# Inverting DeltaNet's 32x32 blocks: rounds of doubling on TensorE in place of a substitution fed through DRAM, with the heads paced

## The chip, the cores and the metric

The kernel runs on one core of a Trainium2 chip. The metric is the device time of one execution in microseconds; the time before is the median of three runs. The profile is that of one execution.

## The reference, cut to what matters

One layer of a diffusion backbone, all in float32: 512 latent tokens and 256 context tokens, width 2048. The tokens are normed and modulated, go through one wide input projection, and feed two mixers of eight heads each. The mixers' results are normed, gated, projected, merged and projected again; a mixture of sixteen experts follows.

The change lies in the second mixer (gated DeltaNet), of which the core is this, for each head and chunk:

```
diff = G[..., :, None] - G[..., None, :]
gamma = jnp.where(incl, jnp.exp(jnp.where(incl, diff, 0.0)), 0.0)
kk = jnp.einsum('bhik,bhjk->bhij', k, k)
m = eye + jnp.where(strict, beta[..., :, None] * kk * gamma, 0.0)
sol = lax.linalg.triangular_solve(m, rhs, left_side=True, lower=True, unit_diagonal=True)
```

What the chunk's state and output need is the inverse of a triangular matrix with ones on its diagonal. The scan runs in both directions, context first.

## The kernel before

The kernel goes through these stages in order: constants and norms; the value projection; per head the first mixer (`hgrn_in`, `hgrn`, with `ada_block` between); then a woven stage with the second mixer's eight heads; `branches` and `merge`; `project`; router; experts.

**The chunks of the second mixer.** The kernel uses chunks of 128 tokens: six (four latent, two context), two directions, so twelve 128x128 triangular matrices N for each head. Their inverse is built in three levels: the 32x32 blocks on the diagonal, then 64x64, then 128x128. The blocks of 32 are kept packed: `uc` (the inverse) and `utc` (its transpose) are tiles of [128, 12, 32], four blocks of 32 rows for each of twelve matrices.

**How a block of 32 is inverted before.** In `gdn_solve`, VectorE packs the 16x16 diagonal blocks into `nk` (two instructions), SyncE's queue stores `nk` to DRAM (`n_d`, 96 KB) and loads it back spread over partitions (`big`, 1536 KB); VectorE then substitutes row by row: 15 times a product `m` and a difference on `ut`. Two scalings by `par` and a transpose give `utc` and `uc` with blocks of 16 inverted. GpSimd has masked `ncm` with `umask`. One step from 16 to 32 follows on TensorE, in the helper `blocks`: 48 small matmuls (32x32 each, every one of two passes in float32, one in each quarter of the array) into a PSUM tile `mx`, copied by ScalarE to `w1`; then two more `blocks`, for `uc` and for `utc`, each subtracted by VectorE.

**The weave.** TensorE's order in this stage is written by the program (`manual_schedule`); the other engines' orders are made by the framework. `weave` holds generators, called streams here: for each head `s_in` (load k, v, q, transposes, norms), `s_solve` (the inverse), two `s_chain` (the scan over six chunks, one for each direction) and `s_out`. A stream yields a distance, or a condition. The distance is counted on `self.pe`, a planner's clock that each matmul moves: `mm` adds its columns, times four in float32, and at least 80, over 2400; `tr` adds 0.107. While no stream is due, one filler step is put in. `fill` gives 640 such steps: 40 products of the input projection (eight `job_gb`, 32 `job_gate`), each 48 matmuls of 512 columns, three to a step (0.64 on the planner's clock). When the filler is used up, the planner's clock jumps to the next due stream and TensorE's order holds nothing in between. The first `pre` filler steps are put ahead of the streams. Filler that is left after the weave is put ahead of the merge, with the loading of its operands (`branches`).

A head's `s_solve` needs its `s_in` and the solve before it; its second half needs the chain before it (`yield free`); a chain needs its solve and the chain before it. The chains of one head thus run beside the next head's solve. The PSUM tiles of solve and chains are all `mx`, of which there are two; the transposes and N use `pcx`, three.

The filler's weights come as `wraw` over SyncE's queue and are split into `whi` (ScalarE) and `wlo` (GpSimd).

Of the kernel before, what the change touches and what calls it, by code (L numbers as in the profile page):

```python
# [8 lines left out]
F32 = mybir.dt.float32  # L9
F32R = mybir.dt.float32r  # L10
I32 = mybir.dt.int32
AF = mybir.ActivationFunctionType
OP = mybir.AluOpType
# [8 lines left out]
H = 8  # L22
# [15 lines left out]
def view(t, off, dims, p0=0, n=128):  # L38
    ps = t.ap[0][0]
    return bass.AP(tensor=t.tensor, offset=t.offset + p0 * ps + off, ap=[[ps, n]] + [list(d) for d in dims])  # L40


class Kern:
# [44 lines left out]
    def consts(self):  # L88
        nc = self.nc
# [3 lines left out]
        tp = self.pool("ctmp", side="right")  # L93
# [3 lines left out]
        def c(name, shape, dt=F32):  # L97
            return (cp if name in late else fp).tile(shape, dt, name=name)

        V = nc.vector  # L100
# [31 lines left out]
        V.tensor_tensor(x32, p31, ii[:, :32], op=OP.bitwise_xor)  # L132
        self.dmask = c("dmask", [128, 32])
        V.tensor_scalar(self.dmask, x32, 0.0, None, op0=OP.is_equal)
        self.lmask = c("lmask", [128, 5, 32], I32)
        t1 = tp.tile([128, 32], F32, name="t1")
        t2 = tp.tile([128, 32], F32, name="t2")
        for n in range(5):
# [1 line left out]
            V.tensor_scalar(t1, x32, float(b), None, op0=OP.is_ge)  # L140
            V.tensor_scalar(t2, x32, float(2 * b), None, op0=OP.is_lt)
            V.tensor_tensor(self.lmask[:, n], t1, t2, op=OP.mult)

        self.umask = c("umask", [128, 32])
        V.tensor_scalar(self.umask, x32, 16.0, None, op0=OP.is_ge)
        self.par = c("par", [128, 2])
        V.tensor_scalar(self.par[:, 1:2], p31[:, 0:1], 16.0, None, op0=OP.is_ge)
        V.tensor_scalar(self.par[:, 0:1], p31[:, 0:1], 16.0, None, op0=OP.is_lt)
        sh2 = tp.tile([128, 16], I32, name="sh2")
        V.tensor_scalar(sh2, pi[:, :16], 15, None, op0=OP.bitwise_and)  # L150
        self.del16 = c("del16", [128, 16])
        V.tensor_tensor(self.del16, sh2, ii[:, :16], op=OP.is_equal)
        self.sel = c("sel", [128, 32])
        V.tensor_tensor(self.sel, p31, ii[:, :32], op=OP.is_equal)

# [230 lines left out]
    def head_norm_steps(self, pool, z, gain, extra, dst, wait=6):  # L386

        nc = self.nc
        V, S = nc.vector, nc.scalar
        sq = pool.tile([128, NL], F32, name="tmp", bufs=4)  # L390
        S.activation(sq, z, AF.Square)
        yield self.opt.get("lm", 1.6)
        pm = self.px.tile([128, NL], F32, name="mx")
        for c in range(4):
            self.mm(pm[:, c:c + 1], sq[:, c * 128:c * 128 + 128], self.ones[:, 0:1])
        ms = pool.tile([128, 4], F32, name="hms")
        rs = pool.tile([128, 4], F32, name="hrs")
        V.tensor_scalar(ms, pm[:, 0:4], 1.0 / 128, EPS, op0=OP.mult, op1=OP.add)
        self.rsqrt(pool, rs, ms)
        yield wait  # L400
        pm = self.px.tile([128, NL], F32, name="mx")
        for c in range(4):
            self.mm(pm[:, c * 128:c * 128 + 128], rs[:, c:c + 1].to_broadcast([128, 128]), self.ident)
        y = sq
        V.scalar_tensor_tensor(y, z, gain, pm, op0=OP.mult, op1=OP.mult)
        if extra is not None:
            V.tensor_tensor(y, y, extra, op=OP.mult)
        nc.scalar.dma_start(dst, y)
# [328 lines left out]
    def gdn_solve(self, h, R, Z, free, after):  # L737
# [2 lines left out]
        V, S, G = nc.vector, nc.scalar, nc.gpsimd  # L740
        kT, qT = R["kT"], R["qT"]
        gm, qe = R["gm"], R["qe"]
        lc = self.opt.get("lc", (2.0, 2.0, 1.6, 4.0, 1.6, 2.5, 1.6, 2.5))
        N = p.tile([128, 2, 6, 128], F32, name="N")
        for i0, w in ((0, 4), (4, 2)):
            pt = self.pt4()
            for i in range(w):
                self.mm(pt[:, i], kT[:, i0 + i], kT[:, i0 + i])
            for d in range(2):
                for i in range(w):  # L750
                    c = i0 + i
                    V.scalar_tensor_tensor(N[:, d, c], pt[:, i], self.beta[:, c, d * 8 + h:d * 8 + h + 1],  # L752
                                           gm[:, d, c], op0=OP.mult, op1=OP.mult)
            yield lc[0]
        P = p.tile([128, 2, 4, 128], F32, name="P", bufs=2)
        pt = self.pt4()
        for i in range(4):
# [4 lines left out]
            self.gdn_decay(after)  # L762
        yield lc[1]

        Nf = N.rearrange("p d c i -> p (d c) i")
        C = lambda n: p.tile([128, 12, 32], F32, name=n)
        ncm, uc, utc, w1 = C("ncm"), C("uc"), C("utc"), C("w1")
        for q in range(4):
            r = slice(32 * q, 32 * q + 32)
            V.tensor_copy(ncm[r], Nf[r, :, r])  # L770
        nk = p.tile([128, 12, 16], F32, name="nk")
        V.tensor_scalar(nk, ncm[:, :, 0:16], self.par[:, 0:1], None, op0=OP.mult)
        V.scalar_tensor_tensor(nk, ncm[:, :, 16:32], self.par[:, 1:2], nk, op0=OP.mult, op1=OP.add)
        nd = self.n_d[h]
        nc.sync.dma_start(nd, nk.rearrange("p c s -> p (c s)"))
        B = p.tile([128, 16, 12, 16], F32, name="big")
        nc.sync.dma_start(B.rearrange("p r c s -> p (r c s)"),
                          bass.AP(tensor=nd.tensor, offset=nd.offset, ap=[[3072, 8], [0, 16], [1, 3072]]))
        ut = p.tile([128, 2, 6, 16], F32, name="ut")
        V.tensor_copy(ut.rearrange("p d c s -> p (d c) s"), self.del16[:, None, :].to_broadcast([128, 12, 16]))  # L780
        m = p.tile([128, 2, 6, 16], F32, name="m")
        for w in range(15, 0, -1):

            mo = m[:, :, :, :w]
            V.tensor_tensor(mo, view(B, w, [[(16 - w) * 192 + 96 + 15 - 2 * w, 2], [16, 6], [192, w]]),
                            view(ut, w, [[96 + 15 - 2 * w, 2], [16, 6], [0, w]]), op=OP.mult)
            uo = view(ut, 0, [[96 + 16 - w, 2], [16, 6], [1, w]])
            V.tensor_tensor(uo, uo, mo, op=OP.subtract)
        utf = ut.rearrange("p d c s -> p (d c) s")
        for a in range(2):  # L790
            V.tensor_scalar(utc[:, :, a * 16:a * 16 + 16], utf, self.par[:, a:a + 1], None, op0=OP.mult)
        fl = lambda t: t.rearrange("p c s -> p (c s)")
        V.transpose(fl(uc), fl(utc))

        nm = ncm
        G.tensor_tensor(nm, ncm, self.umask[:, None, :].to_broadcast([128, 12, 32]), op=OP.mult)

        def blocks(lhs, rhs):
            po = self.ptile("s", [128, 12, 32])
            for i in range(12):  # L800
                for q in range(4):
                    r = slice(32 * q, 32 * q + 32)
                    self.mm(po[r, i], lhs[r, i], rhs[r, i])
            return po

        yield self.opt.get("ls", 32)
        S.activation(w1, blocks(nm, utc), AF.Copy)
        yield lc[2]
        p1 = blocks(w1, uc)
        p2 = blocks(uc, w1)  # L810
        V.tensor_tensor(uc, uc, p1, op=OP.subtract)
        V.tensor_tensor(utc, utc, p2, op=OP.subtract)
        yield lc[3]
        yield free

        U, UT = self.U, self.UT
        w2 = p.tile([128, 6, 32], F32, name="w1")
        pw = self.ptile("s", [128, 6, 32])
        hv = [(d, t + 32 * d, t + 32 * (1 - d)) for t in (0, 64) for d in range(2)]
        for c in range(6):  # L820
# [18 lines left out]
            V.tensor_scalar(UT[i:i + 32, d, :, o:o + 32], p2[i:i + 32], -1.0, None, op0=OP.mult)  # L839
        yield lc[5]  # L840

        w3 = p.tile([128, 6, 64], F32, name="w1")
        pw = self.ptile("s", [128, 6, 64])
        hv = [(d, 64 * d, 64 * (1 - d)) for d in range(2)]
        for c in range(6):
# [13 lines left out]
    def gdn_chain(self, h, d, R, Z, po, seen):  # L859
# [5 lines left out]
        for n in range(6):  # L865
            c = (FWD, BWD)[d][n]
            X = R["vtm"][:, c]
            if n:
                pk = self.ptile("pk", [128, 128])
                self.mm(pk, R["kT"][:, c], st)  # L870
                X = p.tile([128, 128], F32, name="X", bufs=2)
                V.scalar_tensor_tensor(X, pk, self.neG[:, c, hd:hd + 1], R["vtm"][:, c], op0=OP.mult, op1=OP.add)
                yield self.opt.get("lx", 1.0)
            pv = self.ptile("pv", [128, 128])
            self.mm(pv, Z["U"][:, d, c], X)
            a = po[:, c * 128:c * 128 + 128] if c < 4 else None
# [3 lines left out]
            if c < 4:  # L880
# [1 line left out]
                S.activation(vb, pv, AF.Copy, scale=self.beta[:, c, hd:hd + 1])  # L882
                self.mm(a, st, Z["qe"][:, d, c], start=sum(seen) == 0, stop=False)
                seen[c] += 1
            yield self.opt.get("lv", 1.0)
            if n < 5:
                pu = self.ptile("pu", [128, 128])
                self.mm(pu, R["ktm"][:, c], vs)
# [6 lines left out]
            if c < 4:  # L895
                self.mm(a, vb, Z["P"][:, d, c], start=False, stop=seen[c] == 3)
                seen[c] += 1
            yield self.opt.get("lu", 1.0)

    def gdn_out(self, h, po):  # L900
        nc, p = self.nc, self.gp
# [350 lines left out]
    def blocks(self, pr):  # L1252


        w = self.opt.get("lb", (512, 512, 512, 256, 256)) if pr == E // 2 - 1 else (D,)
        return [slice(sum(w[:i]), sum(w[:i + 1])) for i in range(len(w))]
# [207 lines left out]
    def run(self):  # L1464
# [4 lines left out]
        self.y_d = [dp.tile([128, 8, NL], F32, name=f"y_d{i}") for i in range(2)]  # L1469
        self.c_d = [[dp.tile([128, NT + 2], F32, name=f"c_d{h}_{i}") for i in range(3)] for h in range(H)]  # L1470
        self.G_d = dp.tile([16, NT], F32, name="G_d")
        self.n_d = [dp.tile([128, 192], F32, name=f"n_d{i}") for i in range(H)]
        self.mg_d = [dp.tile([128, NL], F32, name=f"mg_d{i}") for i in range(32)]
        self.b_d = [dp.tile([128, NL], F32, name=f"b_d{i}") for i in range(H)]
        self.row_d = [dp.tile([128, D], F32, name=f"row_d{i}") for i in range(2)]
# [43 lines left out]
        filler = self.fill(jobs + gates[3 * len(hs):])  # L1519
        man = self.tc.manual_schedule(engines={mybir.EngineType.PE})  # L1520
        man.__enter__()
        for _ in range(opt.get("pre", 110)):
            next(filler, None)
        n = len(hs)
        did = set()

        def s_in(i):
            yield lambda: i < 1 or ("in", i - 1) in did
            yield from self.gdn_in(hs[i], R[hs[i]], lambda: i < 2 or ("chain", i - 2) in did)
            did.add(("in", i))  # L1530

# [75 lines left out]
```

## Time and profile before

| What | Value |
|---|---|
| median of 3 runs | 3430.93 us (3427.51 to 3434.18) |
| profiled execution | 3427.16 us |
| its span, first to last instruction | 3425.1 us |
| mean granted TensorE clock | 0.963 |
| TensorE busy | 3177.2 us (93%) |
| VectorE busy | 1502.3 us (44%) |
| ScalarE, GpSimd busy | 860.7 us, 367.9 us |

A share of busy time is a mean over stages with different limits. A busy TensorE is not one at its peak: matmuls overlap, so the length of one in the rows (0.39 us for 512 columns) is longer than the distance from one to the next. Float32 matmuls of the streams appear as two records each, one for each pass. In the timeline a bracket at the end of a line gives the idle time ahead of it and what ended that.

### The profile page before, as it was taken

To read this page: it belongs to the slowest core of one execution; us is meant where nothing else is said; L and a number is where in the kernel's file an instruction comes from. 1 tells how busy PE (TensorE), PEld (TensorE's weight loads), DVE (VectorE), ACT (ScalarE), POOL (GpSimd) and SP (SyncE) were. 2 spreads that over 40 slices of the span, in tenths; PEclk is the share of its full clock that TensorE was granted. 3 is DMA by queue.
4 is the path that set the end of the run, shared out by engine and by line. 5 is a ranking of instruction groups with operands and counts; after the bars stand their busy time and mean duration, and the time that the engine had idled before them with its cause. 6 is when DMAs were issued, how large, how long until landed. Compare 5 with 4: busy or idle time off the path is not lost.

```text
span 3425.1 us, 52531 instructions
## 1 busy us (share of the span) xinstructions
PE 3177.2 (93%) x22034; PEld 2301.4 (67%) x22034; DVE 1502.3 (44%) x3101; ACT 860.7 (25%) x1556; POOL 367.9 (11%) x303
## 2 busy tenths in 40 slices
PE   6999999999999989888888779999799999999997
PEld 5788888888888767666766658778544444444443
DVE  5325576676677524455545545423311111211113
ACT  4322323232232224333333322223111010000102
POOL 0000000010000233222222201100000000000002
PEclk9999999999999989899999979999899999999998
DMA  9943264455455435344444325532789999999998
GB/s 305 244 124 117 85 205 152 135 179 159 143 173 166 139 110 135 94 103 103 110 105 110 88 88 151 194 120 71 296 335 420 420 420 420 420 421 420 421 420 308
DMA packets 456268, 738.90 MB, mean 216 GB/s; under 512 B 21723, under 2 KB 332211, under 8 KB 405983
## 3 DMA queue, kind: packets, MB, share of 16 engines
q1 hardware_dynamic: 427503, 688.12, 58.2%
q10 hardware_dynamic: 28528, 47.43, 3.9%
q8 instruction: 173, 2.83, 0.3%
q14 instruction: 64, 0.52, 0.0%
HBM read 703.16 MB, written 32.32 MB: 215 GB/s over the span
## 4 chain that ended last, share of the span: by engine, by line
PE 54%; DMA 7%; DVE 5%; ACT 1%; issue 1%; SPq 0%; ACTq 0%; DVEq 0%
PE pu L80 12%; PE pl L80 11%; PE pg L80 7%; PE px L80 6%; PE po L80 5%; DMA big<-n_d 5%; PE pb L80 5%; PE mx L80 4%; PE py L80 2%; PE pcx L85 1%; DMA rw<-in_router_w 1%; PE pcx L80 1%; DMA yraw<-y_d 0%; DVE N L752 0%; PE lg L80 0%
## 5 line engine op out<-in xcount | busy, mean ns | idle before, releaser
L80 PE MATMUL pl<-hlh,whi 128*128 128x512 f32 (+1 forms) x1552 | 637.1, 411 | 1.7 <-ACT whi L348 1.0
L80 PE MATMUL pl<-hll,whi 128*128 128x512 f32 (+1 forms) x1552 | 617.1, 398 | 0.0
L80 PE MATMUL pl<-hlh,wlo 128*128 128x512 f32 x1536 | 612.9, 399 | 3.7 <-DVE wlo L350 1.8
L348 ACT ACTIVATE whi<-wraw 128x1024 fp32r<-128x1024 f32 (+1 forms) x280 | 289.6, 1035 | 869.5 <-PE pl L80 197.0
L350 DVE TENSOR_TENSOR wlo<-wraw,whi 128x1024 fp32r<-128x1024 f32 (+1 forms) x200 | 256.6, 1284 | 283.9 <-ACT whi L348 283.7
L80 PEld LDWEIGHTS pl<-hlh,whi 128*128 128x128 f32 (+1 forms) x1552 | 295.7, 191 | 59.8 <-ACT whi L348 1.4
L80 PEld LDWEIGHTS pl<-hlh,wlo 128*128 128x128 f32 x1536 | 293.4, 191 | 48.6 <-DVE wlo L350 3.2
L80 PEld LDWEIGHTS pl<-hll,whi 128*128 128x128 f32 (+1 forms) x1552 | 295.6, 190 | 36.0 <-issue 0.7
L80 PE MATMUL pg<-ew,xs 128*64 128x512 f32 x992 | 249.0, 603 | 0.0
L350 POOL TENSOR_TENSOR wlo<-wraw,whi 128x1024 fp32r<-128x1024 f32 x80 | 193.5, 2418 | 490.2 <-ACT whi L348 434.6
L994 DVE SCALAR_TENSOR_TENSOR aacc<-awt,sc,aacc 128x512 f32<-128x512 f32 x256 | 209.6, 819 | 77.0 <-DMA awt<-in_ada_w 68.4
L80 PE MATMUL pu<-ew,xs 128*64 128x512 f32 x1000 | 242.4, 600 | 0.0
L1342 DVE TENSOR_TENSOR xo<-xo,px 128x512 f32<-128x512 f32 (+1 forms) x116 | 76.8, 668 | 360.6 <-PE px L80 360.6
L80 PE MATMUL py<-ew,aa 128*64 128x512 f32 (+1 forms) x608 | 230.1, 583 | 0.0
L80 PE MATMUL pu<-ew,aa 128*64 128x512 f32 x448 | 199.4, 592 | 0.0
L80 PEld LDWEIGHTS pu<-ew,xs 128*64 128x64 f32 x1000 | 88.9, 136 | 122.8 <-issue 115.5
L80 PEld LDWEIGHTS pg<-ew,xs 128*64 128x64 f32 x992 | 87.4, 137 | 120.9 <-issue 112.8
L80 PE MATMUL pcx<-hch,whi 128*128 128x256 f32 (+1 forms) x528 | 149.9, 284 | 0.0
L80 PE MATMUL pcx<-hcl,whi 128*128 128x256 f32 (+1 forms) x528 | 149.0, 282 | 0.0
L80 PE MATMUL pcx<-hch,wlo 128*128 128x256 f32 x512 | 145.8, 285 | 0.0
L80 PEld LDWEIGHTS pu<-ew,aa 128*64 128x64 f32 x448 | 61.5, 137 | 118.3 <-issue 118.3
L80 PEld LDWEIGHTS px<-oh,x 128*128 128x128 f32 x1024 | 125.6, 199 | 7.9 <-DVE xo L1342 4.0
(463 smaller groups left out, 4844.7 us busy)
## 6 DMA issues: line engine op xcount, KB each, us to landing
ew<-in_w_up SPq DMA_DIRECT2D x125, 1024.0 KB
ew<-in_w_gate SPq DMA_DIRECT2D x124, 1024.0 KB
ew<-in_w_down SPq DMA_DIRECT2D x124, 1024.0 KB
wraw<-in_w_in SPq DMA_DIRECT2D x208, 512.0 KB
awt<-in_ada_w SPq DMA_DIRECT2D x128, 512.0 KB
aw<-in_ada_w SPq DMA_DIRECT2D x32, 1024.0 KB
big<-n_d SPq DMA_DIRECT2D x8, 1536.0 KB
wraw<-in_w_out SPq DMA_DIRECT2D x24, 512.0 KB
```

Source lines behind the costliest of these rows:

```text
L80: self.nc.tensor.matmul(out, lhsT, rhs, start=start, stop=stop, skip_group_check=True)
L85: self.nc.tensor.transpose(out, in_, self.ident[:n, :n])
L348: nc.scalar.activation(hi[:, :n], raw[:, :n], AF.Copy)
L350: eng.tensor_tensor(lo[:, :n], raw[:, :n], hi[:, :n].bitcast(F32), op=OP.subtract)
L994: V.scalar_tensor_tensor(acc, w[:, k], self.sc[:, k0 + k, 0:1], acc, op0=OP.mult, op1=OP.add)
L1342: V.tensor_tensor(xo[t][:, cs], (x1 if pr == 0 else xo)[t][:, cs], pz[:, :n], op=OP.add)
```

## The change

The 32x32 blocks are inverted by doubling from 2 to 32. For each level n the part of N that joins two blocks of size 2^n is masked out (`nm[:, n]`; level 0 by VectorE, levels 1 to 4 by GpSimd). Level 0 gives `uc` as identity minus mask, without a product. Each of the four following levels is a round: `blocks(nm[:, n], utc)`, copied by ScalarE to `w1`; `blocks(w1, uc)`, subtracted from `uc` by VectorE, which then transposes `uc` into `utc`. The packing into `nk`, its store, the load of `big`, the substitution and the distance `ls` of 32 are gone. The masks are made ahead of P, where before the packing came behind it.

Beside this, distances are changed: in the solve (`lc`), in the chains (`lx`, `lv`, `lu`) and in the head norm (`lm`). `pre` goes from 110 filler steps to 40. `s_in` of head i also waits until the planner's clock is 70 i past its start.

```diff
@@ consts
-        self.lmask = c("lmask", [128, 5, 32], I32)
+        self.lmask, self.gmask = c("lmask", [128, 5, 32], I32), c("gmask", [128, 5, 32])
...
-        self.umask = c("umask", [128, 32])
-        V.tensor_scalar(self.umask, x32, 16.0, None, op0=OP.is_ge)
-        self.par = c("par", [128, 2])
...
-        V.tensor_tensor(self.del16, sh2, ii[:, :16], op=OP.is_equal)
+            V.tensor_tensor(self.gmask[:, n], t1, t2, op=OP.mult)
@@ head_norm_steps
-        yield self.opt.get("lm", 1.6)
+        yield self.opt.get("lm", 2.2)
@@ gdn_solve
-        lc = self.opt.get("lc", (2.0, 2.0, 1.6, 4.0, 1.6, 2.5, 1.6, 2.5))
+        lc = self.opt.get("lc", (2.4, 4.0, 2.0, 2.6, 2.0, 3.0, 2.0, 3.0))
...
             yield lc[0]
+
+        Nf = N.rearrange("p d c i -> p (d c) i")
+        C = lambda n: p.tile([128, 12, 32], F32, name=n)
+        ncm, uc, utc = C("ncm"), C("uc"), C("utc")
+        for q in range(4):
+            r = slice(32 * q, 32 * q + 32)
+            V.tensor_copy(ncm[r], Nf[r, :, r])
+        nm = p.tile([128, 5, 12, 32], F32, name="nm")
+        fl = lambda t: t.rearrange("p c s -> p (c s)")
+        V.tensor_tensor(nm[:, 0], ncm, self.gmask[:, 0][:, None, :].to_broadcast([128, 12, 32]), op=OP.mult)
+        for n in range(1, 5):
+            G.tensor_tensor(nm[:, n], ncm, self.gmask[:, n][:, None, :].to_broadcast([128, 12, 32]), op=OP.mult)
+
+        V.tensor_tensor(uc, self.dmask[:, None, :].to_broadcast([128, 12, 32]), nm[:, 0], op=OP.subtract)
+        V.transpose(fl(utc), fl(uc))
         P = p.tile([128, 2, 4, 128], F32, name="P", bufs=2)
...
         yield lc[1]
 
-        Nf = N.rearrange("p d c i -> p (d c) i")
-        C = lambda n: p.tile([128, 12, 32], F32, name=n)
-        ncm, uc, utc, w1 = C("ncm"), C("uc"), C("utc"), C("w1")
-        for q in range(4):
-            r = slice(32 * q, 32 * q + 32)
-            V.tensor_copy(ncm[r], Nf[r, :, r])
-        nk = p.tile([128, 12, 16], F32, name="nk")
-        V.tensor_scalar(nk, ncm[:, :, 0:16], self.par[:, 0:1], None, op0=OP.mult)
-        V.scalar_tensor_tensor(nk, ncm[:, :, 16:32], self.par[:, 1:2], nk, op0=OP.mult, op1=OP.add)
-        nd = self.n_d[h]
-        nc.sync.dma_start(nd, nk.rearrange("p c s -> p (c s)"))
-        B = p.tile([128, 16, 12, 16], F32, name="big")
-        nc.sync.dma_start(B.rearrange("p r c s -> p (r c s)"),
-                          bass.AP(tensor=nd.tensor, offset=nd.offset, ap=[[3072, 8], [0, 16], [1, 3072]]))
-        ut = p.tile([128, 2, 6, 16], F32, name="ut")
-        V.tensor_copy(ut.rearrange("p d c s -> p (d c) s"), self.del16[:, None, :].to_broadcast([128, 12, 16]))
-        m = p.tile([128, 2, 6, 16], F32, name="m")
-        for w in range(15, 0, -1):
-
-            mo = m[:, :, :, :w]
-            V.tensor_tensor(mo, view(B, w, [[(16 - w) * 192 + 96 + 15 - 2 * w, 2], [16, 6], [192, w]]),
-                            view(ut, w, [[96 + 15 - 2 * w, 2], [16, 6], [0, w]]), op=OP.mult)
-            uo = view(ut, 0, [[96 + 16 - w, 2], [16, 6], [1, w]])
-            V.tensor_tensor(uo, uo, mo, op=OP.subtract)
-        utf = ut.rearrange("p d c s -> p (d c) s")
-        for a in range(2):
-            V.tensor_scalar(utc[:, :, a * 16:a * 16 + 16], utf, self.par[:, a:a + 1], None, op0=OP.mult)
-        fl = lambda t: t.rearrange("p c s -> p (c s)")
-        V.transpose(fl(uc), fl(utc))
-
-        nm = ncm
-        G.tensor_tensor(nm, ncm, self.umask[:, None, :].to_broadcast([128, 12, 32]), op=OP.mult)
...
-        yield self.opt.get("ls", 32)
-        S.activation(w1, blocks(nm, utc), AF.Copy)
-        yield lc[2]
-        p1 = blocks(w1, uc)
-        p2 = blocks(uc, w1)
-        V.tensor_tensor(uc, uc, p1, op=OP.subtract)
-        V.tensor_tensor(utc, utc, p2, op=OP.subtract)
-        yield lc[3]
+
+        for n in range(1, 5):
+            w1 = p.tile([128, 12, 32], F32, name="w1", bufs=2)
+            S.activation(w1, blocks(nm[:, n], utc), AF.Copy)
+            yield lc[2]
+            V.tensor_tensor(uc, uc, blocks(w1, uc), op=OP.subtract)
+            V.transpose(fl(utc), fl(uc))
+            yield lc[3]
         yield free
@@ gdn_chain
-                yield self.opt.get("lx", 1.0)
+                yield self.opt.get("lx", 1.5)
...
-            yield self.opt.get("lv", 1.0)
+            yield self.opt.get("lv", 1.3)
...
-            yield self.opt.get("lu", 1.0)
+            yield self.opt.get("lu", 1.6)
@@ run
-        for _ in range(opt.get("pre", 110)):
+        for _ in range(opt.get("pre", 40)):
             next(filler, None)
+        t0 = self.pe
...
-            yield lambda: i < 1 or ("in", i - 1) in did
+            yield lambda: i < 1 or ("in", i - 1) in did and self.pe >= t0 + i * opt.get("pace", 70)
```

## Rows read from the trace of the kernel before

**Rows 1.** Stretches by windows: length, busy time and instructions of each engine, TensorE's granted clock, DMA.

```profile
1510.00:1600.00 90.00, 74.07 (x832) 61.74 (x831) 51.31 (x148) 32.83 (x68) 22.56 (x10) 0.92 0.41 106
1960.00:2050.00 90.00, 63.70 (x714) 51.70 (x714) 46.05 (x131) 26.06 (x48) 0.00 (x0) 0.71 0.24 80
2050.00:2140.00 90.00, 89.91 (x397) 74.47 (x398) 46.67 (x44) 23.02 (x26) 12.34 (x9) 1.00 0.52 152
```

**Rows 2.** The chain that ended last, in order of time: start, length, what.

```profile
1166.68 26.12 PE pl L80 x115
...
1321.72 22.18 DMA big<-n_d
...
1943.35 16.48 DMA big<-n_d
```

**Rows 3.** Waits of TensorE, 1281 to 1947 us: total, times, longest.

```profile
PE mx L80 <- DVE X L872: 63.2, 10, 11.2
PE mx L80 <- issue: 12.0, 7, 2.9
PE mx L80 <- DVE S L891: 8.6, 7, 2.5
PE mx L80 <- ACT w L823: 3.1, 3, 1.7
PE pl L80 <- POOL wlo L350: 1.7, 1, 1.7
```

**Rows 4.** Waits of VectorE in the same stretch.

```profile
DVE m L785 <- DMA big<-n_d: 76.3, 7, 12.4
```

**Rows 5.** Timelines of VectorE and TensorE around one such wait: start, length, instruction.

```profile
1519.08 0.46 DVE L785 TENSOR_TENSOR m<-big,ut 128x180 f32<-128x180 f32 x1 [10.47 <-DMA big<-n_d]
...
1520.24 0.80 PE L80 MATMUL mx<-X,U 128*128 128x128 f32 x2 [9.26 <-DVE X L872]
...
1524.74 0.39 PE L80 MATMUL po<-P,vb 128*128 128x128 f32 x2
```

**Rows 6.** TensorE's timeline: one `blocks`, what follows it, and the end of three.

```profile
1549.15 1.02 PE L80 MATMUL mx<-utc,ncm 32*32 32x32 f32 x96
1550.10 0.88 PE L85 MATMUL pcx<-ident,ktm 128*128 128x128 f32 x6
...
1556.96 0.28 PE L80 MATMUL mx<-w,uc 32*32 32x32 f32 x10 [2.93 <-issue]
```

**Rows 7.** By tile: count, shortest, median and longest in ns, first and last start.

```profile
L811 DVE TENSOR_TENSOR uc<-uc,mx x8: 553/554/555, 1376.2 to 1979.4; 128x384 f32<-128x384 f32 x8
L793 DVE STREAM_TRANSPOSE uc<-utc x8: 566/572/581, 1358.9 to 1973.7; 128x384 f32<-128x384 f32 x8
L807 ACT ACTIVATE w<-mx x8: 490/492/492, 1368.2 to 1975.4; 128x384 f32<-128x384 f32 x8
L796 POOL TENSOR_TENSOR ncm<-ncm,umask x8: 994/1017/1027, 1319.7 to 1941.3; 128x384 f32<-128x384 f32 x8
L688 DVE TENSOR_TENSOR ktm<-ktm,rsk x8: 957/958/3197, 1288.7 to 1899.2; 128x768 f32<-128x768 f32 x8
```

**Rows 8.** The last head of the first mixer: VectorE's timeline; filler by windows (first TensorE).

```profile
1212.56 0.30 DVE L494 COPY_PREDICATED sd<-lmask,mx 128x128 f32<-128x128 int32 x1 [5.09 <-PE mx L80]
...
1200.00:1230.00 30.00, 28.31 (x118) 21.86 (x118) 0.69 (x1) 1.74 (x3) 0.99 0.33 96
1230.00:1260.00 30.00, 25.52 (x105) 19.35 (x105) 0.00 (x0) 1.18 (x2) 1.00 0.37 107
```

**Rows 9.** The end of the weave: last filler by tile; TensorE and the merge's products by windows.

```profile
L80 PE MATMUL pl<-hlh,wlo x1536: 387/394/794, 246.2 to 1947.6; 128*128 128x512 f32 x192
...
1948.68:2025.11 76.43, 42.52 (x647) 0.65 0.16 44
...
2025.00:2051.00 26.00, 22.97 (x78) 16.74 (x79) 2.05 (x3) 0.84 0.59 199
2051.00:2100.00 49.00, 49.00 (x218) 40.58 (x217) 6.19 (x9) 1.00 0.55 161
```

**Rows 10.** Waits of TensorE, 1947 to 2051 us.

```profile
PE mx L80 <- DVE X L872: 12.2, 1, 12.2
PE mx L80 <- DVE uc L811: 0.6, 1, 0.6
PE mx L80 <- ACT w L807: 0.6, 1, 0.6
```

More of the change, by code (lines that the diff above doesn't have):

```diff
@@ L142, in consts @@
             V.tensor_tensor(self.lmask[:, n], t1, t2, op=OP.mult)
-        self.umask = c("umask", [128, 32])
-        V.tensor_scalar(self.umask, x32, 16.0, None, op0=OP.is_ge)
-        self.par = c("par", [128, 2])
[L147 to L151, printed above, removed]
-        V.tensor_tensor(self.del16, sh2, ii[:, :16], op=OP.is_equal)
+            V.tensor_tensor(self.gmask[:, n], t1, t2, op=OP.mult)
         self.sel = c("sel", [128, 32])
@@ L804, in blocks @@
             return po
-        yield self.opt.get("ls", 32)
-        S.activation(w1, blocks(nm, utc), AF.Copy)
-        yield lc[2]
-        p1 = blocks(w1, uc)
-        p2 = blocks(uc, w1)
-        V.tensor_tensor(uc, uc, p1, op=OP.subtract)
-        V.tensor_tensor(utc, utc, p2, op=OP.subtract)
-        yield lc[3]
+        for n in range(1, 5):
[5 more added lines that the diff above has]
+            yield lc[3]
         yield free
         U, UT = self.U, self.UT
-        w2 = p.tile([128, 6, 32], F32, name="w1")
+        w2 = p.tile([128, 6, 32], F32, name="w1", bufs=2)
         pw = self.ptile("s", [128, 6, 32])
@@ L840, in gdn_solve @@
         yield lc[5]
-        w3 = p.tile([128, 6, 64], F32, name="w1")
+        w3 = p.tile([128, 6, 64], F32, name="w1", bufs=2)
         pw = self.ptile("s", [128, 6, 64])
@@ L1471, in run @@
         self.G_d = dp.tile([16, NT], F32, name="G_d")
-        self.n_d = [dp.tile([128, 192], F32, name=f"n_d{i}") for i in range(H)]
         self.mg_d = [dp.tile([128, NL], F32, name=f"mg_d{i}") for i in range(32)]
```

## The prediction

> **What bounds the kernel now.** I read the page first, then stretches by windows, then what TensorE waits for in the stretch that is changed. Around it TensorE is full: right behind the weave it is busy for 89.91 of 90 us at a granted clock of 1.00, while a head's 90 us in the weave have it busy for 74.07 at 0.92, and the weave's last 90 us for 63.70 at 0.71 [rows 1]. So inside the weave TensorE is the engine that counts, but it is held up: by waits, and by the half clock (1.2 of 2.4 GHz) behind them.
>
> The waits say by what. From 1281 to 1947 us TensorE stands 63.2 us for VectorE's X, a step of the chains, in ten pieces; the next are 12.0 us of issue and 8.6 us for S [rows 3]. VectorE is not busy then: it waits seven times, 76.3 us in all, for `big` to land [rows 4]. The timelines show how one becomes the other. The product `m` stands at the head of VectorE's queue for 10.47 us, the chain's X is queued behind it, TensorE's order is fixed and waits 9.26 us for X; then a pair of passes takes 0.80 us, and 0.39 us only from 1524.74 on [rows 5]. The chain that ended last runs through the eight loads of `big`, between 16 and 23 us each, of which the first and the last stand in [rows 2].
>
> Two more losses lie at the ends. The last filler is done at 1947.6 us, and from there to the merge's first product TensorE has 42.52 us of work at a clock of 0.65 in 76.43 us [rows 9]. Ahead of the weave, filler stands in TensorE's order between the levels of the first mixer's last head: VectorE waits 5.09 us for a product each time [rows 8].
>
> **The parts, with their costs.** A filler product takes 26.12/115 = 0.227 us [rows 2], a step of three 0.68.
>
> *The load is removed.* Seven of the ten X waits belong to it; at some 8.3 us each (9.26 in the one shown) that is 58 of the 63.2 us [rows 3, 5]. From 1520.24 to 1524.74 TensorE ran at half clock, which costs half of that, 2.2 us, seven times: 15 us. Gain 73. The eighth wait of the kind (12.2 us [rows 10]) is counted with the tail below. SyncE's two issues a head go too; nothing on the path waits for that queue. VectorE loses 30 substitution steps and the packing, and gets per round a difference (0.55 us) and a transpose (0.57) [rows 7]: less work than before, on an engine that is busy for 51 of 90 us [rows 1].
>
> *Blocks are added.* Three `blocks` a head become eight. One is 96 passes in 1.02 us, and the next instruction starts 0.95 us behind its start [rows 6]. Five more, eight heads: 40 x 0.95 = 38 us on a full TensorE. The price could be lower only if they filled idle time (0), and higher by fetching: today 12.0 us of issue waits [rows 3] fall on 24 blocks, all late in a run of blocks, as the one of 2.93 us [rows 6]. At 0.5 us a block, 64 blocks would have 32 us, 20 more; spaced out by filler, as each now is, perhaps none, 12 less. I take no change.
>
> A rule speaks against this price. The Trainium skill, "TensorE: Matmul & The Clock Gate", section on the clock gate, says that matmuls never start less than about 25 ns apart, however narrow. By it the 96 passes would take 2.4 us and the forty blocks 96 us; the trace disagrees, with 96 passes in 0.95 us, about 10 ns apart.
>
> *Hops.* A round has two: block, ScalarE's copy (0.49 us), block; block, difference and transpose (1.12 us on VectorE), block [rows 7]. 64 hops in all. The distances 2.0 and 2.6 become four and five filler steps, 2.7 and 3.4 us, so work and semaphore fit if the engines come at once. What doesn't fit: an engine that is busy with another stream, and the two `mx` tiles, which the chains share. From below: covered hops of this kind cost 3.1 us in all on `w` over eight heads [rows 3], some 0.1 each. From above: uncovered ones in the tail cost 0.6 [rows 10]. I take 0.25, near the covered ones: 64 x 0.25 = 16 us, between 6 and 42.
>
> *Longer distances in the chains* cover part of the 8.6 us for S and of what is left on X: gain 4, between 0 and 12.
>
> *Does the filler last?* On the planner's clock a head's solve has matmuls of 29.0 (ten of 0.213, eight blocks of 48 x 0.0533, 6.4 in the two upper levels) and distances of 37.2; whole steps of 0.64 round these up by 7, collisions add some 3: 76 a head. The first `s_in` takes 30, the last chain 36, the last `s_out` 27: the streams end at 30 + 608 + 63 = 701. The work is 600 steps of 0.64 plus 8 x 43 (29.0, chains 10.2, `s_in` 2.8, `s_out` 1.0) = 728. So 27 units, some 42 steps or 29 us, are left behind the streams, and the merge's loads (some 25 us) run beside them. The same count for the kernel before gives 581 of work against some 687: filler out long before the end, as the trace has it. Pacing at 70 does not bind, since the solve takes 76.
>
> *The tail* then goes. Of 76.43 us, 42.52 at 0.65 are 28 us of work at full clock, 48 lost; behind it 78 merge products take 26 us where 49/218 = 0.225 us each would give 17.5, 8.5 lost [rows 9]. Together 57, of which I leave 5: gain 52.
>
> *The filler that pays for it* comes from ahead of the weave. Of 357 early products (110 steps, and nine put in while k loads) 147 remain, and 115 of these fit where they ran before, in 26.12 us [rows 2]. Between the levels stand 118 + 105 = 223 products, 50.6 us of 60 [rows 8]. About 190 of them, 43 us, move into the weave. That is no loss by itself if the last head of the first mixer gets as much faster. It doesn't quite: its levels hand over between VectorE, ScalarE and TensorE, with VectorE's work about 1 us each. Some ten gaps of 20 to 25 products at 1.4 us are 14 us of new idle time; the bounds are 0 and 43.
>
> *At nothing:* three more masks on GpSimd (1.0 us each [rows 7]), which is a quarter busy (22.56 of 90 us [rows 1]) and holds TensorE up for 1.7 us in all [rows 3]; without that cover, 3 us a head. P comes 3 us later on VectorE, behind the masks, and is read only by the chain, a solve later; behind P the next head's `gm` load, which has the solve as cover. The constants are a few small instructions before any product.
>
> **Sum.** Gains 73 + 4 + 52 = 129; costs 38 + 16 + 14 = 68; net 61. The profiled execution took 3427.2 us, 3.8 less than the median; both are moved by the same 61, so 3366 for such an execution and 3370 us for the median. What comes behind the merge starts earlier by as much and is unchanged.
>
> **Rivals.**
>
> *Hops become the bound (slower).* At each of the 64 hops TensorE, in its fixed order, waits behind VectorE's queue. For it: VectorE has pieces that last up to 3.2 us where 0.96 is usual [rows 7], and rounds now run beside the chains of the head before. Against: covered hops were almost free. From (16 + 61)/64 = 1.2 us a hop the change is no gain; at 2 us it is 128 - 16 = 112 us more than forecast, 3482.
>
> *The filler runs out early.* The planner counts 2.56 for a block that takes 0.95 us, and collisions may stretch the solve: 27/8 = 3.4 units a head more and the surplus is gone. The tail stays half (3396) or whole (3422).
>
> *The first mixer's last head doesn't shorten.* If it is held by its own steps and not by filler, the 43 us are bought dearly: 29 worse, 3399. Against: every gap there is a wait for TensorE [rows 8].
>
> *The blocks cost what the 25 ns rule says:* 58 more, 3428. The 0.95 us of [rows 6] speaks against it.
>
> *All fits better:* hops at 0.1, issue waits gone, new idle time near 5: about 3338.
>
> **Chances and range.** Forecast 0.47, its own range 3348 to 3393; hops 0.08; filler out 0.17; last head 0.13; 25 ns 0.03; better 0.12. I take 3335 to 3415 us, which leaves out the slower rival, the rule, the worst of the filler and a little below: under 2 in 10. Faster by over 0.2% (about what a measurement tells from no change) 0.87; within 0.2% 0.05; slower 0.08.
>
> **What the profile after would show.** No wait of VectorE on `big`, and X waits of TensorE below 10 us; a head's 74 us or so instead of 90; blocks still 0.95 us apart; waits behind `w` and `uc` of some 16 us; filler still running when the last chain ends, so that the merge follows at full clock near 1970 us; the levels of the first mixer's last head some 2 to 3 us apart instead of 6. I would be wrong if TensorE stood for `uc` or `mx` over a microsecond a hop, if filler ended before the last solve, or if the weave's start did not come forward by some 30 us.

## The result, and the profile after

The changed kernel takes 3369.18 us (median of four runs, 3368.48 to 3372.12) against 3432.35 us before; the ratio is 0.9821, with a 95% interval from 0.9809 to 0.9833. The forecast was 3370 us, and a gain of 61; the medians differ by 63.2.

One thing about the two profiled executions. The last head of the first mixer starts its scores at 1206.5 us after and at 1199.9 us before, and nothing ahead of that point bears on the change. All thirteen other executions profiled here, of kernels of both kinds, reach it between 1206.0 and 1210.1 us: the execution of before was some 7 us early there. From that point to the merge's last product it takes 1007.4 us before (to 2207.3) and 946.4 us after (to 2152.9): 61.0 us less. The two stretches as windows (busy time and instructions of TensorE, its weight loads, VectorE, ScalarE, GpSimd; TensorE's granted clock, DMA share, GB/s), before first:

```profile
1199.90:2207.30 1007.40, 857.07 (x7930) 708.00 (x7921) 503.67 (x1326) 338.01 (x643) 224.61 (x106) 0.91 0.41 111
1206.50:2152.90 946.40, 882.07 (x11768) 727.76 (x11759) 447.39 (x1110) 349.46 (x666) 251.89 (x130) 0.97 0.36 105
```

TensorE's idle time falls by 86.0 us (150.3 to 64.3), and its busy time grows by 25.0.

Shorter stretches of the changed kernel in the same form, to be held against [rows 1]:

```profile
1500.00:1590.00 90.00, 85.59 (x1372) 71.44 (x1367) 49.80 (x148) 35.54 (x74) 29.17 (x15) 0.98 0.31 89
...
1880.00:1947.00 67.00, 67.00 (x346) 56.96 (x345) 14.16 (x40) 17.74 (x26) 23.96 (x10) 1.00 0.37 100
```

TensorE is now busy for 85.59 of 90 us in the weave, and the weave's end, which stood at a clock of 0.71, is filled: 67.00 of 67 us. Its waits from 1254 to 1972 us (total, times, longest):

```profile
PE pcx L85 <- DMA acc<-c_d: 10.9, 1, 10.9
PE mx L80 <- DVE X L845: 8.3, 5, 2.0
PE mx L80 <- ACT w L782: 6.8, 11, 3.8
PE mx L80 <- DVE UT L812: 5.3, 6, 1.6
...
PE mx L80 <- DVE uc L784: 0.9, 4, 0.2
PE mx L80 <- DVE S L864: 0.8, 2, 0.4
PE mx L80 <- ACT w L796: 0.6, 1, 0.6
PE mx L80 <- issue: 0.5, 1, 0.5
```

The first line's wait ends with the weave's first product, at 1253.6 us; the kernel before has one like it, 11.3 us, that ends at 1280.2, just ahead of the stretch of [rows 3]. The five groups of [rows 3] had 88.6 us; the same five have 17.0 now (8.3 + 0.5 + 0.8 + 7.4 + 0, with both lines of `w` in the 7.4). The X waits that are left are of 2.0 us at most.

By tile, the first transpose of each head (count, shortest, median and longest in ns, first and last start):

```profile
L760 DVE STREAM_TRANSPOSE utc<-uc x8: 560/564/566, 1293.8 to 1818.6; 128x384 f32<-128x384 f32 x8
```

A head takes (1818.6 - 1293.8)/7 = 75.0 us. Before, the transpose of [rows 7] gives (1973.7 - 1358.9)/7 = 87.8. The masks, in the view of their tile:

```profile
L757 POOL TENSOR_TENSOR nm<-ncm,gmask x32: 990/1170/1382, 1290.9 to 1819.2; 128x384 f32<-128x384 f32 x32
L755 DVE TENSOR_TENSOR nm<-ncm,gmask x8: 558/1644/2094, 1290.8 to 1814.1; 128x384 f32<-128x384 f32 x8
```

GpSimd's four a head are little longer than the one of [rows 7]; VectorE's, of the same size, takes 0.56 us at best and 1.64 in the median. It starts beside GpSimd's first (1290.8 and 1290.9 us in the first head); that this is the cause was not tried.

One of the new groups on TensorE's timeline, with what stands ahead of it and behind:

```profile
1596.01 0.39 PE L80 MATMUL pl<-hll,whi 128*128 128x512 f32 x1
1596.24 0.40 PE L80 MATMUL pl<-hlh,wlo 128*128 128x512 f32 x1
1596.57 1.02 PE L80 MATMUL mx<-utc,nm 32*32 32x32 f32 x96
1597.52 0.49 PE L80 MATMUL mx<-vs,ktm 128*128 128x128 f32 x2
```

It is 0.95 us from its start to the next one's, as in [rows 6]. But the filler product ahead of it takes 0.33 us until the group starts, where 0.23 is usual. In the median, such a product took 0.32 us (20 groups), and a filler product behind a group 0.34 (7 groups). The first mixer's last head on VectorE's timeline, where [rows 8] had 5.09 us of waiting at each level:

```profile
1215.72 0.30 DVE L485 COPY_PREDICATED sd<-lmask,mx 128x128 f32<-128x128 int32 x1 [0.86 <-PE mx L80]
...
1217.54 0.30 DVE L485 COPY_PREDICATED sd<-lmask,mx 128x128 f32<-128x128 int32 x1 [0.86 <-PE mx L80]
```

The levels stood some 6.1 us apart (1200.35 to 1224.67 in four steps) and now stand 1.8 to 4.1 apart. And the end of the weave in the chain that ended last:

```profile
1918.75 25.95 PE pl L80 x114
1957.08 6.22 DMA yraw<-y_d
1964.71 4.44 DMA yraw<-y_d
1971.58 181.75 PE pb L80 x768
```

Filler runs through the last chain and output, and the merge's 768 products follow after a wait of 2.8 us (`mg`); [rows 9] had 76.43 us at a clock of 0.65 there. The merge's products themselves became a little longer (by tile, before and after: shortest, median and longest in ns):

```profile
L80 PE MATMUL pb<-yl,whi x256: 388/389/794, 2025.9 to 2207.1; 128*128 128x512 f32 x128
L80 PE MATMUL pb<-yl,whi x256: 392/397/628, 1971.9 to 2152.7; 128*128 128x512 f32 x128
```

The median of 397 stands in every run of the changed kernel and its variants, 389 in every run of the kernel before and its variants, at a granted clock of 1.00 from 2100 us on in both profiles. With 768 products that is some 6 us; why they are longer is not shown.

### The profile page after: what moved, and what is told of

Read it like the earlier page. It is cut to its first block, busy times and chain, and to the rows that moved or that the text cites. A ratio compares the mean times of both kernels' runs of the same rounds, so it can differ in the third digit from the quotient of the medians.

```text
span 3367.6 us, 60040 instructions
## 1 busy us (share of the span) xinstructions
PE 3202.7 (95%) x25874; PEld 2316.7 (69%) x25874; DVE 1446.2 (43%) x2885; ACT 871.8 (26%) x1580; POOL 395.0 (12%) x327
## 4 chain that ended last, share of the span: by engine, by line
PE 46%; DVE 3%; DMA 2%; ACT 1%; issue 1%; ACTq 0%; SPq 0%; DVEq 0%
PE pu L80 12%; PE pg L80 7%; PE px L80 6%; PE pb L80 5%; PE po L80 5%; PE pl L80 5%; PE mx L80 2%; PE py L80 2%; DMA wraw<-in_w_out 1%; DMA ew<-in_w_gate 0%; DMA yraw<-y_d 0%; DMA gm<-G_d 0%; PE lg L80 0%; ACT xs L1271 0%; PE pt L85 0%
## 5 line engine op out<-in xcount | busy, mean ns | idle before, releaser
L80 PEld LDWEIGHTS pg<-ew,xs 128*64 128x64 f32 x992 | 84.5, 137 | 122.9 <-issue 114.4
```

The costliest lines, as they stand in the source:

```text
L80: self.nc.tensor.matmul(out, lhsT, rhs, start=start, stop=stop, skip_group_check=True)
```

## The experiments

Each was compared with the kernel before on the same chip, four runs each (ten for the wide products). Before was 3433 to 3436 us in these comparisons. The changed kernel was timed in the comparison above alone, so differences from it go by its 3369.18 us.

**The schedule alone.** The kernel before with `pre` 40, the pace, and the longer distances of the chains, the norms and the solve (`lc[3]` stays 4.0):

```diff
-        lc = self.opt.get("lc", (2.0, 2.0, 1.6, 4.0, 1.6, 2.5, 1.6, 2.5))
+        lc = self.opt.get("lc", (2.4, 4.0, 2.0, 4.0, 2.0, 3.0, 2.0, 3.0))
...
```

> The kernel before, with the substitution through DRAM kept, and only the schedule changed: 40 filler steps ahead, pace 70, the longer distances in chains, norms and solve. If the gain is the sum of the removed load waits (73 us), the covered tail (52) and the added costs, the load waits stay, about 63 us of TensorE's waits for X; the filler lasts some 39 planner's units longer and gives back some 35 us of the tail, less 14 us of idle time ahead of the weave: about 3410 us. Rival, that the schedule alone makes the gain and the load is hidden by it: about 3370. Second rival, that the schedule is worth nothing without the new inverse: 3430.

It took 3460.41 us, ratio 1.0072 (1.0052 to 1.0091): slower. Its waits for X:

```profile
PE mx L80 <- DVE X L872: 77.5, 9, 13.8
```

The load waits stay, as expected. The rest of the expectation missed: I had left out that the solve's longer distances (five units a head by the code) stretch every head; as the only cause they were not tried. Heads stand (2004.6 - 1333.7)/7 = 95.8 us apart instead of 87.8, and the filler, with 70 steps more, still ends 85 us ahead of the merge's first load of the weave's results (1968.0 against 2052.7).

**The inverse alone.** The changed kernel with `pre` 110, no pace, and the old distances in chains and norms; the solve keeps its longer distances, which belong to the rounds:

```diff
...
-        for _ in range(opt.get("pre", 40)):
+        for _ in range(opt.get("pre", 110)):
...
-            yield lambda: i < 1 or ("in", i - 1) in did and self.pe >= t0 + i * opt.get("pace", 70)
+            yield lambda: i < 1 or ("in", i - 1) in did
```

> The changed kernel with the schedule of before: 110 filler steps ahead, no pace, the old distances in chains and norms; the new inverse stays. By the sum: no load waits; 683 planner's units of work against some 695 for the streams, so the filler is out a little before the end, and the last head's output and the merge's loads are uncovered again, some 25 us; 14 us of idle time ahead of the weave are saved; chains wait some 4 us more: about 3384. Rival, that the schedule makes the gain: 3420 or more.

3370.10 us, ratio 0.9812 (0.9795 to 0.9830): all of the gain. By tile, the filler's last product, and the merge's:

```profile
L80 PE MATMUL pl<-hlh,wlo x1536: 387/395/797, 248.9 to 1962.1; 128*128 128x512 f32 x192
...
L80 PE MATMUL pb<-yh,wlo x256: 390/397/628, 1965.3 to 2152.4; 128*128 128x512 f32 x128
```

The tail is covered without the 70 steps: filler to 1962.1, the merge from 1965. The 25 us that I had expected there did not come. Waits for S are up (16.2 us against 0.8), which is what the longer distances in the chains give; in the whole time that doesn't show.

**Without the load.** The kernel before, with `big` a tile of zeros that is written once, ahead of the heads; the store of `nk` stays:

```diff
+        self.B = p.tile([128, 16, 12, 16], F32, name="big")
+        self.nc.gpsimd.memset(self.B, 0.0)
...
-        B = p.tile([128, 16, 12, 16], F32, name="big")
-        nc.sync.dma_start(B.rearrange("p r c s -> p (r c s)"),
-                          bass.AP(tensor=nd.tensor, offset=nd.offset, ap=[[3072, 8], [0, 16], [1, 3072]]))
+        B = self.B
```

> The kernel before without the load of the spread-out tile: the substitution reads zeros that were written once, so the inverse of the blocks of 16 is the identity; everything else, the store to DRAM and the distance of 32 too, stays. If the load itself is the wait, X waits of TensorE fall from 63 us to some 5, the half clock behind them goes (15 us) and the tail loses its own 12 us: about 3345. Rival, that the wait only moves, since the 30 steps of the substitution then hold VectorE's queue up instead: X waits of 30 us or more and about 3390.

3347.79 us, ratio 0.9747 (0.9732 to 0.9762): 87 us less, and 3.4 us of X waits left:

```profile
PE mx L80 <- DVE X L872: 3.4, 3, 1.8
```

The 30 steps of the substitution are no obstacle on VectorE. So the load, with what hangs on it, is worth some 87 us, and the new inverse pays some 20 of them back.

**Every group twice.** The changed kernel, in `blocks`:

```diff
+            for rep in range(2):
+                pe = self.pe
                 for i in range(12):
...
+                if rep:
+                    self.pe = pe
```

> The changed kernel with every group of 48 small products issued twice into the same tile, the planner's clock held for the second, so that the order stays: 64 groups more. At 0.95 us each on a full TensorE: 61 us more, about 3430. By the rule of at least 25 ns between starts: 2.4 us each, 154 us more, about 3523. If groups fill idle time of the hops: under 30 us more. If instruction fetch binds when groups stand together, issue waits of 20 us or more come on top of the 61.

3560.01 us, ratio 1.0360 (1.0332 to 1.0388): 191 us, or 3.0 for each of the 64 groups. Both prices of the prediction miss; the last of the four expectations came, waits on issue on top of the 61: 90 us, where 20 or more were named. TensorE's waits show why, from 1254 to 2150 us:

```profile
PE mx L80 <- issue: 83.4, 42, 2.8
...
PE pl L80 <- issue: 3.8, 3, 1.8
PE po L80 <- issue: 3.0, 2, 1.9
```

and its timeline, with 192 passes that break off at 150:

```profile
1503.76 1.47 PE L80 MATMUL mx<-utc,nm 32*32 32x32 f32 x150
1507.68 0.57 PE L80 MATMUL mx<-utc,nm 32*32 32x32 f32 x42 [2.45 <-issue]
```

The page's queues of the two kernels, first the changed one:

```profile
q8 instruction: 203, 3.33, 0.4%
```

```profile
q8 instruction: 251, 4.11, 0.5%
```

64 groups of 96 passes with 96 weight loads are 12,288 instructions; they came as 48 packets more, 256 to a packet of 16 KB. The waits on issue, 47 of them with 90.2 us against one of 0.5, are 1.9 us for each packet more. The rest shows in the windows of the weave, the doubled groups first:

```profile
1253.00:2150.00 897.00, 779.21 (x16858) 652.38 (x16858) 338.72 (x977) 295.37 (x593) 227.73 (x112) 0.93 0.28 79
1253.00:1972.00 719.00, 680.49 (x10716) 565.16 (x10717) 338.95 (x976) 295.22 (x597) 228.10 (x112) 0.98 0.34 98
```

The profiled execution is one of 3547.88 us, and its weave is 178 us longer: 79 of idle time, in which other waits shrank beside the 90, and 99 of busy time, of which 64 x 0.93 = 60 are work and the other 39 go with the lower clock, 0.93 instead of 0.98.

**Wide work of the same length.** To part instructions from TensorE's time: six products of 384 columns ahead of each group instead of a second group.

```diff
+            pe = self.pe
+            for _ in range(6):
+                self.mm(po.rearrange("p c s -> p (c s)"), self.hlh[:, 0, :128], self.hlh[:, 0, :384])
+            self.pe = pe
```

> The changed kernel with six wide products (384 columns, one pass each, 12 instructions in all) ahead of each group of 48 small ones, into the same tile, the planner's clock held: about as much time on TensorE as a second group (0.93 us), with 12 instructions instead of 192. The run with groups issued twice cost 191 us, 3.0 us for each of 64. If that was the supply of instructions, this one costs 64 x 1.0 = 65 us, 3435, with issue waits under 5 us. If it was TensorE's time or waits for the tile, it costs as much as the doubled groups, 3540 or more.

3434.64 us: 65 us more than the changed kernel, as expected. On TensorE's timeline the six take 1.24 us and the group behind them 0.95:

```profile
1500.22 1.31 PE L80 MATMUL mx<-hlh 128*128 128x384 f32 x6
1501.46 1.02 PE L80 MATMUL mx<-uc,w 32*32 32x32 f32 x96
1502.41 0.66 PE L85 MATMUL pcx<-ident,accq 128*128 128x128 f32 x4
```

No wait on issue is left in the weave. With the same time and 12 instructions instead of 192, the waits are gone: the doubled groups were dear by their instructions.

**Hops without cover.** `lc[2]` and `lc[3]` set to 0:

```diff
-        lc = self.opt.get("lc", (2.4, 4.0, 2.0, 2.6, 2.0, 3.0, 2.0, 3.0))
+        lc = self.opt.get("lc", (2.4, 4.0, 0.0, 0.0, 2.0, 3.0, 2.0, 3.0))
```

> The changed kernel with the two distances of a round set to 0, so that nothing but what is due anyway stands between a group of products and the next one that needs its result. If filler is what hides the hops, waits on w and uc come up, 64 of about 0.6 us and more: 30 to 80 us slower, 3400 to 3450, and waits on issue rise too, since groups stand closer together. Rival, that the chains hide them just as well, or that earlier solves give back what the waits cost: 3370.

3490.53 us, ratio 1.0169 (1.0154 to 1.0184): 121 us more than the changed kernel, beyond what I expected.

```profile
PE mx L80 <- DVE utc L785: 44.3, 31, 2.2
PE mx L80 <- ACT w L782: 30.3, 20, 6.0
PE mx L80 <- issue: 13.0, 17, 1.8
```

```profile
1253.00:1903.00 650.00, 530.67 (x9697) 451.99 (x9697) 293.67 (x912) 237.47 (x517) 161.92 (x84) 0.84 0.26 73
1903.00:2092.00 189.00, 184.35 (x1020) 151.87 (x1021) 36.62 (x74) 58.03 (x83) 66.92 (x28) 0.97 0.46 133
```

75 us stand behind `utc` and `w`, 1.2 a hop, and the clock over the weave is 0.84 instead of 0.98. The 190 us behind it are filler that was not there to cover the hops.

**The pace, and `pre` by itself.** Two single edits of the changed kernel: the pace taken out, and `pre` at 110.

> The changed kernel without the pace of 70. If the solve, of 76 planner's units a head, sets the heads' distance, the pace never binds behind the first two heads: 3369 within 4 us. Rival, that the pace keeps the filler for the end: 10 us or more slower.

> The changed kernel with 110 filler steps ahead instead of 40, all else kept. After the run with the whole old schedule came out the same as the changed kernel, the theory is that idle time ahead of the weave and filler at its end trade one for one: 3370 within 5 us. Rival, by the sum that was forecast (52 us of tail against 14 ahead): 3385 or more.

3373.33 and 3375.36 us: 4 and 6 more than the changed kernel, at the edge of what can be told apart. Neither rival came (10 us or more; 3385 or more). With 110 steps ahead the last filler product starts at 1957.4 us and the merge's first at 1970.0, so the tail is covered but for 12.6 us.

**The substitution held back.** The load's wait can be taken from VectorE's queue in another way. In the kernel before, the substitution's start value goes through a product with the identity, placed some planner's units behind the load, so that VectorE's order has the chains' X first:

```diff
-        V.tensor_copy(ut.rearrange("p d c s -> p (d c) s"), self.del16[:, None, :].to_broadcast([128, 12, 16]))
+        yield self.opt.get("lh", 20)
+        pz = self.ptile("s", [128, 12, 16])
+        self.mm(pz, self.ident, self.del16[:, None, :].to_broadcast([128, 12, 16]))
+        V.tensor_copy(ut.rearrange("p d c s -> p (d c) s"), pz)
...
-        yield self.opt.get("ls", 32)
+        yield self.opt.get("ls", 16)
```

> The kernel before with its trip through DRAM and its substitution, but the substitution held back: its start value goes through one product of TensorE that stands 20 planner's units behind the load, and the distance ls is 16 instead of 32. VectorE's queue then has the chains' X ahead of the substitution. If the price of the trip was only that the load stood at the head of VectorE's queue, the X waits go (63 us to some 5, and 15 us of half clock) and the long tail stays, since the filler is used up as before: 3350 to 3375, as fast as the changed kernel or faster. Rival, that the trip itself, 20 us a head, is on the path: 3410 or more.

> The same with the product 16 units behind the load and a distance ls of 11, so 27 units for load and substitution instead of 32: five units less a head. If the load has landed by then and the tail is what is left, the filler lasts some 40 us longer into it: 15 to 30 us faster than with 20 and 16, about 3340. If 16 units are too short for the load, X waits of 3 us and more a head come back: no faster.

With 20 and 16 units: 3394.63 us, ratio 0.9882 (0.9867 to 0.9897), more than I expected. With 16 and 11: 3368.23 us, ratio 0.9805 (0.9789 to 0.9822), as fast as the changed kernel. The planned wait of 32 units is 36 in the first and 27 in the second, so the first has the new order on VectorE with four units a head more, the second with five less. Heads stand 81.3 us apart in the first and 77.2 in the second (87.8 before). In the first, the view of the tile `big`: what its readers' engine stood idle for (us, times).

```profile
its engine sat idle before it (us, times) until:
  DMA big<-n_d: 1.5, 1
```

And TensorE's waits in it, from 1250 to 2150 us:

```profile
PE mx L80 <- DVE utc L794: 28.1, 8, 12.5
...
PE mx L80 <- DVE X L875: 4.2, 6, 1.7
```

With 16 and 11 the X waits are:

```profile
PE mx L80 <- DVE X L875: 7.8, 7, 1.8
```

The load takes as long as before where the chain that ended last shows it (16.8 us in the first; 23.3 and 19.4 in the second), but hardly anything waits for it: 1.5 us where [rows 4] had 76.3, and 4.2 us of X waits. What is left is the substitution's end (`utc`), and the tail: from the last filler product to the merge's first it is 114.4 us with 20 and 16 (from 1882.3), 35.1 with 16 and 11 (from 1937.1), 77.5 before. So the new order alone gives 40 us against a longer tail, and the other 26 come with the shorter solve. Two more tried to cover that tail with `pre` 40, the first with 16 and 11, the second with 15 and 14:

> The kernel with the substitution held back by 16 and 11 units (3368 us, as the changed kernel), with 40 filler steps ahead instead of 110. Its filler ran out at 1937 us and its merge reached full clock at 1996; with 70 steps more in the weave the tail, some 34 us lost, is covered, and the idle time ahead of the weave, some 15 us, is paid: about 3350, faster than the changed kernel. Rival, that early and late filler trade one for one, as they did in the changed kernel: 3365 to 3372.

> The same with 15 and 14 units: the 34 us that TensorE waited for the end of the substitution (eight times 4.2) should shrink to some 10, and the filler is used up some 16 us earlier: 3340 to 3355. Rival, that the solve's length is what counts, so that two units more a head cost 16 us: 3365.

3385.81 us (ratio 0.9857, 0.9843 to 0.9872), slower than with 110 steps ahead, and 3365.94 us (0.9795, 0.9778 to 0.9811). The second can't be told from the changed kernel; no version tried here clearly beats both. Why 16 and 11 lose 18 us when 70 steps of filler are moved into the weave stays open: its trace has one wait of 9.8 us for the filler's `whi` that was not there before, but the run with 15 and 14 has one of 10.3 as well.

## Why the prediction was right, point by point

*The load.* Right, and shown twice: without it (3348), and with it but out of VectorE's way (3395 with four units a head more, 3368 with five less). The X waits fell by 55 us where 58 were forecast.

*Blocks.* The distance of 0.95 us came out as forecast, and nothing of 25 ns between starts. The Trainium skill's rule ("TensorE: Matmul & The Clock Gate", the clock gate) holds in no run here: passes of four quarters start 10 ns apart. But the term was booked too low. The products ahead of and behind a group lose some 0.1 us each (0.32 and 0.34 instead of 0.23), which for forty groups is 8 us more than the 38, an estimate from the groups counted above. And the price is not a constant: in the run with every group twice, one more group of 192 instructions cost 3.0 us.

*Issue.* I took no change between 12 less and 20 more; 12.0 us became 0.5. Groups with filler between them are fed in time; three in a row were not.

*Hops.* Forecast 16 us; `w` and `uc` have 7.7, or 0.12 a hop, near the lower bound. Without cover they cost 1.2 each in waits alone, just the point at which the slower rival was to decide, and the kernel was slower than before. That is not yet the rival, which had hops wait behind VectorE's other work in spite of the distances; what is shown is that the distances of 2.0 and 2.6 are what hides the hops.

*Chains' distances.* Forecast 4; the waits for S fell from 8.6 to 0.8. The run with the inverse alone has 16.2 and is as fast, so that in the whole time this term can't be seen.

*The tail, and the filler that pays for it.* Here the step failed, though the sum held. The text lets the 52 us be bought with the 70 steps taken from ahead of the weave, at 14 us. Two of its parts came out: the tail is covered, with some 23 us of filler behind the weave's last product (1945.6 to 1968.4; 29 were forecast), and ahead of the weave TensorE is idle for 26.4 us where it was idle for 15.6, 10.8 more. But the tail did not need the 70 steps. Without them, the count of the same kind had the filler out early and 25 us lost; the filler ran to 1962.1, and 3370.10 us came out. With the longer distances and `pre` at 110, some 6 us are lost. Moving the 70 steps gave back about what it cost.

Why the filler lasts is argued, not shown. Filler by windows of a head's length, after and before:

```profile
1443.00:1518.00 75.00, 41.90 (x158) 27.90 (x158) 0.00 (x0) 1.76 (x3) 1.00 0.31 86
1446.00:1534.00 88.00, 54.42 (x195) 35.95 (x195) 0.68 (x1) 2.36 (x4) 0.92 0.42 107
```

Before has some 195 products a head (65 steps), after some 158 (53), so twelve steps of 0.68 us, 8 us a head, are left for the end. The planner's clock points the same way, if further: it books 2.56 for a group that takes 0.95 us, and five groups more fill 12.8 units of a head, twenty steps, that filler filled before.

*The head's length.* Forecast 74 us, measured 75.0. The weave started 27 us earlier in the profiled executions, 33 when the early point of before is allowed for; "some 30" was forecast. The merge started at 1971.6 (granted clock 0.97 over its first 50 us); full clock was forecast near 1970.

The sum fits better than its terms: hops and issue came out some 20 us cheaper than booked (16 - 7.7 and 12.0 - 0.5). The two profiles show what takes these back. In idle time and half clock the text booked 129 - 16 - 14 = 99 us. Measured are 86.0 of idle time and, as an estimate, 26 of half clock (busy time times the missing share of the clock, in windows of 1 us: 47.7 before, 21.5 after), 112 in all. Against that, TensorE's work at full clock grew by 25.0 + 26 = 51 us and not by 38: the 8 us beside the groups and the 6 us of the merge, a stage taken as unchanged, make up the difference. So two misses of some 13 us cancel, and the hit to within 2 us is luck; either miss alone would have left the time inside the range.

## What to carry to other kernels

A wait at the head of an in-order queue costs what stands behind it, not what it is for: read who is queued behind it before the transfer itself is replaced, since a small dependence that moves the waiting work back, with a solve planned five units shorter, did as much here as a new algorithm. Small matmuls on parts of the array are priced by two things, their time and their instructions; keep wide work between groups of them. And a schedule written on a planner's clock changes when the clock's prices are off: count the filler that a stage uses up, not the units.

## What the runs showed of the hardware

TensorE's instructions arrive in packets of 16 KB, 256 instructions to a packet (48 packets more for 12,288 instructions, 0.78 MB). The Trainium skill, "Runtime: NRT & Kernel Launch", section on instruction fetch, says the same of the blocks, and that crossing from one to the next is mostly hidden. The trace agrees on the size; with 96 passes and 96 weight loads in 0.95 us, and some 3 us of other work between groups, it is hidden (0.5 us of waits in the weave), and with twice as many it isn't: 90.2 us in 47 waits, 1.9 us for each packet more.
